# Three edits to the feed-forward stage of a one-core decoder layer: the rate of weight sums in DRAM, the place of one gate product, the order of one group of matrix products

## The chip, the core and the metric

The kernel is one program on one core of a Trainium2 chip. Five engines work side by side, each through its own instructions in order: TensorE (PE, matrix products; its weight loads are PEld), VectorE (DVE), ScalarE (ACT), GpSimd (POOL) and SyncE (SP, which here only issues transfers). Sixteen DMA engines move data between DRAM and the on-chip memory, and from DRAM to DRAM. The metric is the device time of one execution in microseconds (us); lower is better. Three executions of the kernel before took 1026.02, 1028.47 and 1030.43 us; the median is 1028.47 us.

## What is computed

One decoder layer on 512 tokens of 1024 channels in float32: a recurrent mixer and an attention mixer, merged by gates, and then a gated feed-forward block with a short convolution over time. The edits lie in the feed-forward block, which is this part of the reference:

```python
up = causal_dwconv(rms_norm(x, norm2_g) @ w_up, ffn_conv_w, ffn_conv_b)
gate, val = jnp.split(up, 2, axis=-1)
x = x + (jax.nn.gelu(gate) * val) @ w_down
```

Here x is 512 x 1024, w_up is 1024 x 6144, gate and val have 3072 channels each, and w_down is 3072 x 1024. The convolution has three taps per channel.

## The kernel before

**Precision.** Every float32 operand is split into a rounded high part and a remainder (whi and wlo of a weight tile wraw, xh and xl of an activation), and a product is three matrix products: high by high, high by low, low by high. ACT makes the high part (line 202 for weights, line 264 for activations) and DVE the remainder (line 210 and line 265). So PE can't start the first product of a weight tile before ACT's copy, nor the third before DVE's subtraction. PE's order is written out by hand in this stage; the order on the other engines is set by a scheduler when the program is built, and at run time each engine keeps to that order: an instruction that waits holds up all that stands behind it.

**The up product.** The 3072 gate channels are 24 chunks of 128, and so are the value channels. Chunks 0 to 5 are done as plain products. Chunks 6 to 23 (the Strassen part) are done with a seven-product scheme on 2 x 2 blocks: gate and value of a chunk are the two block rows, the two halves of the 1024 input channels the inner blocks, 256 tokens a block column. `seed(j)` does four of the products (weight tiles u1 and u2 of chunk j), `rest(j)` the other three (u3 and u4), and the PE order is seed(j+1), rest(j), seed(j+2), and so on. Block sums of activations (b11, t1 to t4, b21, b22) are made once; block sums of weights are not made by an engine, but in DRAM: `sums()` copies the blocks of chunk j into a DRAM tile ws (line 1267, issued by SP) and then adds to it three times by accumulating transfers (line 1270, issued by POOL). The down product needs sums too, in twelve DRAM tiles dn0 to dn11, one for each pair of chunks: one copy of 512 KB (line 1292, SP), then an accumulating transfer from the input "we" and one from dn to itself, 256 KB each (line 1270, POOL). Each of POOL's accumulating transfers waits for the transfer before it on the same tile to land.

**When the sums are issued.** `sums()` is a generator of steps; a copy is one step, the two or three accumulating transfers of a round are the next. `_wprep`, which issues the load of each weight tile in the order of a plan of 229 tiles (line 196, SP), takes further steps by a table: with SUM_RATE's entry (116, 1.2), one step for 1.2 weight tiles up to tile 116, after that one for 2.4. The Strassen part begins at tile 109 of the plan. A step is issued behind the load of its tile on SP.

**From up to down.** For each chunk, `conv` applies the taps (ACT line 1349, DVE line 1352) into two tiles y (four buffers), ACT applies the gelu (line 1451), and `gated` multiplies the two into f (line 1361): chunks 0 to 7 lie in f0, 8 to 15 in fxh, 16 to 23 in fxl. POOL does these products, in the same queue as its accumulating transfers, except the last one (chunk 23), which DVE does. `down_ops(n)` makes the operands of pair n, which joins chunks k and k + 4 (pair 3 joins 3 and 7): sums dt on DVE (lines 1494 to 1496), then the split into dh and dl. Pair 3 has a buffer of its own for dt, and the scheduler has put its DVE instructions into the Strassen part.

**The down product** has two phases. In phase one each of the 12 pairs gives four kinds of product (`one`, kinds a, c, d, e) into four output groups p = 0 to 3 (two PSUM banks each: r0 with halves lo and hi, r1 with halves lo and hi). Then `mix(p)` combines the four halves of a group: ACT copies r0 to ad, and DVE does four additions in place (lines 1555 to 1558; 1556 writes r0 hi, 1557 writes r1 lo, 1558 reads r1 lo and writes r1 hi). In phase two `two(p, n)` adds three more products for each pair: c into r1 lo, d into r0 hi, a into r0 lo.

Of the kernel before, what the change touches and what calls it, by code (L numbers as in the profile page):

```python
# [25 lines left out]
FC = D_FF // 128  # L26
# [37 lines left out]
    return k, k + 4  # L64


SUM_AT, SUM_RATE = 20, ((43, 0.65), (54, 2.0), (80, 4.0), (116, 1.2), (999, 2.4))
WLEAD = 2
ACC1, ACC2 = (0, 1, 2, 5, 8, 11), (0, 1, 2, 5, 8)

# [59 lines left out]
class Kern:  # L130
# [1207 lines left out]
    def ffn(self):  # L1338
        nc, ff = self.nc, self.ff
# [3 lines left out]
        fs = lambda j: f[j // 8][:, j % 8]  # L1343
# [11 lines left out]
        def plain(c):  # L1355
            ps = self.up0.pop(0) if self.up0 else self.proj("up", c)
            nc.vector.tensor_mul(ps, ps, self.rstd)
            return conv(ps, c)

        def gated(j, yg, yv):  # L1360
            (nc.vector if j == FC - 1 else nc.gpsimd).tensor_mul(fs(j), yg, yv)


        SB = {}
# [78 lines left out]
        def rest(j, r0, r1):  # L1443

            w = self.w("u3", j, WLEAD)
            prod(r0[:, 256:512], w, 0, "b22")
            prod(r0[:, 0:256], w, 512, "b21")
            w = self.w("u4", j, WLEAD)
            prod(r1[:, 0:256], w, 0, "t4")
            yg = conv(r0, j)  # L1450
            nc.scalar.activation(yg, yg, AF.Gelu_apprx_tanh)
            gated(j, yg, conv(r1, FC + j, True))

        with tp("xt", side="right") as xt:
            x = xt.tile([128, KO, S], F32, name="xs")
            steps = prep(x, xt)
            for j in range(NPL):
                yg = plain(j)
                nc.scalar.activation(yg, yg, AF.Gelu_apprx_tanh)
                next(steps, None)  # L1460
                gated(j, yg, plain(FC + j))
                next(steps, None)
            for _ in steps:
                pass
# [48 lines left out]
    def down(self, fs, first):  # L1513

        nc, fo = self.nc, self.fo
        N, lo, hi = FC // 2, slice(0, 256), slice(256, 512)
        banks = [self.ps.tile([128, S], F32, name="mm", bufs=self.mmb) for _ in range(7)]
        banks.append(self.ps.tile([128, S], F32, name="misc"))
        r = [(banks[i], banks[j]) for i, j in ((0, 1), (2, 3), (4, 7), (5, 6))]
        self.down_load(2)  # L1520
        X = {0: first, 1: self.down_ops(1, fs)}
        W = {}

        def mm(ps, w, o, x, i, start=False, stop=False):
            c = slice(o, o + 128)
            nc.tensor.matmul(ps, w[0][:, c], x[0][:, i], start=start, stop=False, skip_group_check=True)  # L1526
            nc.tensor.matmul(ps, w[0][:, c], x[1][:, i], start=False, stop=False, skip_group_check=True)  # L1527
            nc.tensor.matmul(ps, w[1][:, c], x[0][:, i], start=False, stop=stop, skip_group_check=True)  # L1528

        def get1(n):  # L1530
            if n not in X:
                X[n] = self.down_ops(n, fs)
            W[n] = self.w("d1", n, WLEAD), self.w("d2", n, WLEAD)

        def one(p, n, which="acde"):
            (w1, w2), x, (r0, r1), o = W[n], X[n], r[p], 128 * p
            last = n == N - 1
            for s in which:
                if s == "a":
                    mm(r0[:, lo], w1, o, x, 0, n == 0, last)  # L1540
                elif s == "c":
                    mm(r1[:, lo], w1, 512 + o, x, 1, n == 0, last)
                elif s == "d":
                    mm(r0[:, hi], w2, 512 + o, x, 2, False, last)
                else:
                    mm(r1[:, hi], w2, o, x, 3, False, last)

        def mix(p):
            r0, r1 = r[p]
            a, d, c, e = r0[:, lo], r0[:, hi], r1[:, lo], r1[:, hi]  # L1550
            with self.tc.high_priority(HPRI):
                ad = fo.tile([128, S], F32, name="ad", bufs=2)
                ac = fo.tile([128, 256], F32, name="ac", bufs=2)
                nc.scalar.copy(ad, r0)
                nc.vector.tensor_tensor(ac, c, ad[:, lo], ALU.add)
                nc.vector.tensor_tensor(d, d, ac, ALU.add)
                nc.vector.tensor_tensor(c, e, ac, ALU.add)
                nc.vector.tensor_tensor(e, c, ad[:, hi], ALU.add)  # L1558

        def get2(n):  # L1560
            X[n] = self.down_ops2(n, fs)
            w4 = self.w("d4", n, WLEAD)
            W[n] = self.w("d3", n, WLEAD), w4

        def two(p, n, which="cda"):
            (w3, w4), x, (r0, r1), o = W[n], X[n], r[p], 128 * p
            last = n == N - 1
            for s in which:
                if s == "d":
                    mm(r0[:, hi], w3, o, x, 1, False, last)  # L1570
                elif s == "a":
                    mm(r0[:, lo], w3, 512 + o, x, 0, False, last)
                else:
                    mm(r1[:, lo], w4, o, x, 2, False, last)

        def store(p, j, cs):
            m = p + 4 * j
            o = self.ff.tile([128, S], F32, name="y", bufs=4)
            for c in cs:
                if j:  # L1580
                    nc.vector.tensor_sub(o[:, c], self.xn[:, m, c], r[p][1][:, c])  # L1581
                else:
                    nc.vector.tensor_add(o[:, c], r[p][0][:, c], self.xn[:, m, c])  # L1583
                nc.sync.dma_start(self.out[:, m, c], o[:, c])

        get1(0)
        for p, which in ((0, "ac"), (1, "ac"), (2, "c"), (0, "de"), (1, "de"), (2, "ade")):
            one(p, 0, which)
        get1(1)
        for p, n in ((0, 1), (1, 1), (3, 0), (2, 1), (3, 1)):  # L1590
            one(p, n)
        for n in range(2, N):
            get1(n)
            for p in range(4):
                one(p, n)
                if n == N - 1:
                    mix(p)
        for n in range(N - 2):
            get2(n)
            for p in range(4):  # L1600
                two(p, n)
        get2(N - 2)
        two(0, N - 2)
        two(1, N - 2)
        get2(N - 1)
        for p in range(3):
            two(p, N - 1)
            store(p, 0, (slice(0, S),))
            store(p, 1, (slice(0, S),))
            if p < 2:  # L1610
                two(p + 2, N - 2)
        for s in "cda":
            two(3, N - 1, s)
            if s == "c":
                store(3, 1, (slice(0, S),))
        store(3, 0, (hi, lo))
# [174 lines left out]
```

## Time and profile before

The profiled execution took 1027.07 us in all, and its span from the first to the last instruction is 1025.3 us.

| | before |
|---|---|
| median of three executions | 1028.47 us |
| profiled execution / its span | 1027.07 / 1025.3 us |
| busy share: PE, PEld, DVE, ACT, POOL | 98%, 87%, 79%, 63%, 27% |
| mean granted TensorE clock | 0.994 |
| transfers issued by SP (queue q1) | 153.65 MB |
| transfers issued by POOL (queue q0) | 30.98 MB |

A row of the timeline reads: start in us, duration in us, engine, line, operation, out<-in, count, and in brackets how long the engine had been idle and what released it. A row of the waits reads: who waits, for whom, us in total, times, longest. A row of the stretches gives for each engine the busy time and the count of instructions in the stretch, then the granted TensorE clock (PEclk, 1.00 is full), the busy share of the 16 DMA engines (it can pass 1 by a little) and GB/s. "DMA to landing" is the time from the issue of a transfer to its completion. Lines are those of the kernel before.

### The profile page before, as it was taken

How to read it: one execution, taken by the hardware profiler on the slowest of the kernel's cores; microseconds unless marked ns; L12 is line 12 of the kernel's file. 1: busy time of each engine (PE TensorE's matmuls, PEld its weight loads, DVE VectorE, ACT ScalarE, POOL GpSimd, SP SyncE). 2: the span in 40 equal slices, each digit the busy share in tenths (PEclk: the TensorE clock that was granted, in tenths of full speed). 3: DMA queues.
4: the chain of work that ended last, by engine and by line, in shares of the span. 5: the costliest groups of instructions: out<-in, count | busy, mean ns of one | idle time of the engine just before them, and what ended most of it. 6: DMA issues, size and time to landing. Idle time of an engine off the chain costs nothing. (4 is left out here: it accounts for less than half of the span.)

```text
span 1025.3 us, 16991 instructions
## 1 busy us (share of the span) xinstructions
PE 1005.7 (98%) x6089; PEld 895.6 (87%) x6089; DVE 807.7 (79%) x1569; ACT 645.8 (63%) x1075; POOL 273.8 (27%) x350
## 2 busy tenths in 40 slices
PE   9999999999999999999999999999989999999998
PEld 7888888988888888888888878888989999999997
DVE  6868879788778687769598564599678888899876
ACT  6466776878867663578787543465446666665553
POOL 0155335334443400341332004234211111221000
PEclk9999999999999999999999999999999999999999
DMA  7534654665656677763645978668976656786553
GB/s 250 113 89 105 169 146 131 162 152 157 185 144 165 191 250 232 179 206 126 168 112 148 302 207 226 165 184 236 274 201 195 191 185 200 207 229 203 156 185 124
DMA packets 74933, 185.88 MB, mean 181 GB/s; under 512 B 18011, under 2 KB 19675, under 8 KB 71008
## 3 DMA queue, kind: packets, MB, share of 16 engines
q1 hardware_dynamic: 66064, 153.65, 45.0%
q0 software_dynamic: 8640, 30.98, 17.9%
q8 instruction: 48, 0.79, 0.3%
q14 instruction: 37, 0.30, 0.1%
q10 hardware_dynamic: 144, 0.15, 0.1%
HBM read 175.53 MB, written 57.93 MB: 228 GB/s over the span
## 5 line engine op out<-in xcount | busy, mean ns | idle before, releaser
L202 ACT CAST whi<-wraw 128x1024 fp32r<-128x1024 f32 (+3 forms) x178 | 177.9, 999 | 148.6 <-PE mm L1419 50.7
L210 DVE TENSOR_TENSOR wlo<-wraw,whi 128x1024 fp32r<-128x1024 f32 (+2 forms) x145 | 166.0, 1145 | 60.3 <-ACT whi L202 60.1
L239 PE MATMUL mm<-xh,whi 128*128 128x512 f32 x456 | 178.8, 392 | 0.0
L241 PE MATMUL mm<-xh,wlo 128*128 128x512 f32 x456 | 178.6, 392 | 0.0
L240 PE MATMUL mm<-xl,whi 128*128 128x512 f32 x456 | 178.3, 391 | 0.0
L207 POOL TENSOR_TENSOR wlo<-wraw,whi 128x256 fp32r<-128x256 f32 (+1 forms) x131 | 94.9, 777 | 100.7 <-ACT whi L202 82.3
L241 PEld LDWEIGHTS mm<-xh,wlo 128*128 128x128 f32 x456 | 85.6, 188 | 18.5
L239 PEld LDWEIGHTS mm<-xh,whi 128*128 128x128 f32 x456 | 85.7, 188 | 16.8
L240 PEld LDWEIGHTS mm<-xl,whi 128*128 128x128 f32 x456 | 85.7, 188 | 16.7
L929 ACT ACTIVATE s<-s,bs,rq 128x128 f32<-128x128 f32 (+3 forms) x128 | 82.4, 647 | 13.8 <-DVE bs L926 13.7
L1527 PE MATMUL mm<-dl,whi 128*128 128x256 f32 x300 | 84.0, 280 | 1.6 <-DVE dl L265 1.6
L1526 PE MATMUL mm<-dh,whi 128*128 128x256 f32 x300 | 84.0, 280 | 1.5 <-DVE mm L1558 1.5
L1528 PE MATMUL mm<-dh,wlo 128*128 128x256 f32 x300 | 83.9, 280 | 0.0
L265 DVE TENSOR_TENSOR ptl<-T,pth 128x512 fp32r<-128x512 f32 x80 | 55.0, 688 | 20.7 <-ACT pth L264 19.8
L264 ACT CAST pth<-T 128x512 fp32r<-128x512 f32 x80 | 46.2, 582 | 31.8 <-PE T L958 31.2
L1270 POOL DMA_DIRECT2D ws<-ws x36 | 28.5, 791 | 137.8 <-DMA ws<-in_wi 63.8
L922 DVE CUSTOM_DVE_ANT_0 s<-S,cc 128x128 f32<-128x128 f32 (+3 forms) x128 | 58.1, 482 | 2.8 <-PE S L919 2.4
L1527 PEld LDWEIGHTS mm<-dl,whi 128*128 128x128 f32 x300 | 56.5, 188 | 2.0 <-DVE dl L265 2.0
L1526 PEld LDWEIGHTS mm<-dh,whi 128*128 128x128 f32 x300 | 56.4, 188 | 1.9 <-DVE mm L1558 1.7
L1528 PEld LDWEIGHTS mm<-dh,wlo 128*128 128x128 f32 x300 | 56.4, 188 | 0.2 <-DVE wlo L210 0.2
L958 PE MATMUL T<-cc,s 128*128 128x128 f32 x320 | 48.2, 273 | 0.6 <-DVE s L934 0.6
L958 PEld LDWEIGHTS T<-cc,s 128*128 128x128 f32 x320 | 39.5, 140 | 10.2 <-DVE s L934 0.8
(439 smaller groups left out, 2874.1 us busy)
## 6 DMA issues: line engine op xcount, KB each, us to landing
wraw<-in_w SPq DMA_DIRECT2D x102, 512.0 KB, 3.6
ws<-in_wi SPq DMA_DIRECT2D x36, 512.0 KB, 5.0
wraw<-ws SPq DMA_DIRECT2D x72, 256.0 KB, 3.3
wraw<-in_w SPq DMA_DIRECT2D x54, 256.0 KB, 3.2
ws<-in_wa POOLq DMA_DIRECT2D x18, 512.0 KB, 6.0
ws<-ws POOLq DMA_DIRECT2D x36, 256.0 KB, 4.8
dn<-in_wd SPq DMA_DIRECT2D x12, 512.0 KB, 5.9
ds<-in_w SPq DMA_DIRECT2D x24, 256.0 KB, 3.4
```

The costliest lines, as they stand in the source:

```text
L202: self.last_hi = nc.scalar.copy(hi[:, :n], raw[:, :n])
L207: nc.gpsimd.tensor_sub(lo[:, e], raw[:, e], hi[:, e].bitcast(F32))
L210: self.last_lo = nc.vector.tensor_sub(lo[:, :e], raw[:, :e], hi[:, :e].bitcast(F32))
L239: nc.tensor.matmul(ps, wh, xh, start=first, stop=False)
L240: nc.tensor.matmul(ps, wh, xl, start=False, stop=False)
L241: nc.tensor.matmul(ps, wl, xh, start=False, stop=last)
L922: nc.vector.tensor_tensor_reduce(s[i, x], ps[:, x - xs[0]], mask, 1.0, -3e38, ALU.add, ALU.max, mx[:, x, i:i + 1])
L929: self.last_exp = nc.scalar.activation(s[t, x], s[t, x], AF.Exp, bias=bs[:, x, t:t + 1], scale=rq[:, t], accum_out=sm[:, x, t:t + 1])
L958: nc.tensor.transpose(T[:, off:off + 128], s[i, x][:, 128 * j:128 * j + 128], self.ident)
L1526: nc.tensor.matmul(ps, w[0][:, c], x[0][:, i], start=start, stop=False, skip_group_check=True)
L1527: nc.tensor.matmul(ps, w[0][:, c], x[1][:, i], start=False, stop=False, skip_group_check=True)
L1528: nc.tensor.matmul(ps, w[1][:, c], x[0][:, i], start=False, stop=stop, skip_group_check=True)
```

## The change

There are three edits. The steps of the sums are taken at 1.3 weight tiles a step up to tile 116 and at 2.8 after it, instead of 1.2 and 2.4. The gate product of chunk 23 is not issued on DVE where it is ready, but behind the remainder of the weight tile that is the latest when pair 2 of phase one is fetched (`issue_after` makes the scheduler place it behind that instruction). And in phase two, pair 0's products of each group run in the order a, d, c instead of c, d, a.

```diff
-SUM_AT, SUM_RATE = 20, ((43, 0.65), (54, 2.0), (80, 4.0), (116, 1.2), (999, 2.4))
+SUM_AT, SUM_RATE = 20, ((43, 0.65), (54, 2.0), (80, 4.0), (116, 1.3), (999, 2.8))
...
         def gated(j, yg, yv):
-            (nc.vector if j == FC - 1 else nc.gpsimd).tensor_mul(fs(j), yg, yv)
+            if j == FC - 1:
+                self.last_f = lambda: nc.vector.tensor_mul(fs(j), yg, yv)
+            else:
+                nc.gpsimd.tensor_mul(fs(j), yg, yv)
...
         for n in range(2, N):
             get1(n)
+            if n == 2:
+                with self.tc.issue_after(self.last_lo.ins):
+                    self.last_f()
             for p in range(4):
                 one(p, n)
...
             get2(n)
             for p in range(4):
-                two(p, n)
+                two(p, n, "cda" if n else "adc")
```

The three places below show how this moves instructions. Numbers behind a name tell buffers apart and differ between the two programs; in dn10 and ws10 the first number is that of the pair or chunk. Lines of the changed kernel are up to six higher.

First SP, in the Strassen part, where chunk 10's tiles are loaded. Before:

```order
L196 DMA wraw_7770<-in_w 128x512
L1292 DMA dn11_7774<-in_wd 16x8192
L196 DMA wraw_7809<-in_w 128x512
L196 DMA wraw_7809<-ws10_2506 128x512
L196 DMA wraw_7840<-ws10_2506 128x512 x2
```

and with the change:

```order
L196 DMA wraw_7766<-in_w 128x512
L196 DMA wraw_7803<-in_w 128x512
L196 DMA wraw_7803<-ws10_2506 128x512
L1292 DMA dn10_7808<-in_wd 16x8192
L196 DMA wraw_7836<-ws10_2506 128x512 x2
```

The copy for dn11 stood two transfers before chunk 10's first block sum; now the copy for dn10 stands behind it, and dn11's comes ten loads further on. The copies ahead of this place have moved by one pair: at about the places of dn7 to dn10 stand dn6 to dn9 now.

Second POOL, at the end of the same stretch, from the accumulating transfers of the last pairs to the first products of fxh. Before:

```order
L1361 TENSOR_TENSOR f0_6921<-y_7593,y_7598 128x512
L1270 DMA dn10_7640<-dn10_7640 32x2048
L1270 DMA dn11_7774<-in_we 32x2048
L1270 DMA dn11_7774<-dn11_7774 32x2048
L1361 TENSOR_TENSOR f0_6921<-y_7727,y_7732 128x512
L1361 TENSOR_TENSOR fxh_7378<-y_7859,y_7864 128x512
```

and with the change:

```order
L1364 TENSOR_TENSOR f0_6919<-y_7589,y_7594 128x512
L1270 DMA dn9_7636<-dn9_7636 32x2048
L1270 DMA dn10_7808<-in_we 32x2048
L1364 TENSOR_TENSOR f0_6919<-y_7723,y_7728 128x512
L1270 DMA dn10_7808<-dn10_7808 32x2048
L1364 TENSOR_TENSOR fxh_7374<-y_7855,y_7860 128x512
L1270 DMA dn11_8004<-in_we 32x2048
L1270 DMA dn11_8004<-dn11_8004 32x2048
```

The second product into f0 (chunk 7) stood behind three accumulating transfers after chunk 6's; it now stands behind two.

Third DVE, at the start of phase one of the down product. Before:

```order
L1494 TENSOR_TENSOR dt_9924<-f0_6921 128x256
L1361 TENSOR_TENSOR fxl_7379<-y_9762,y_9767 128x512
L1495 TENSOR_TENSOR dt_9924<-f0_6921 128x256
L1494 TENSOR_TENSOR dt_10071<-fxh_7378 128x256
L1496 SCALAR_TENSOR_TENSOR f0_6921<-dt_9924,f0_6921 128x256
L1495 TENSOR_TENSOR dt_10071<-fxh_7378 128x256
L210 TENSOR_TENSOR wlo_9857<-dg_9780,whi_9856 128x1024
L210 TENSOR_TENSOR wlo_9861<-ds_9781,whi_9860 128x1024
L265 TENSOR_TENSOR dl_9926<-f0_6921,dh_9925 128x512
L210 TENSOR_TENSOR wlo_9943<-dg_9798,whi_9942 128x1024
L265 TENSOR_TENSOR dl_9926<-dt_9924,dh_9925 128x512
```

and with the change, from the fifth of these on:

```order
L1498 TENSOR_TENSOR dt_10071<-fxh_7374 128x256
L265 TENSOR_TENSOR dl_9925<-dt_9923,dh_9924 128x512
L1499 SCALAR_TENSOR_TENSOR fxh_7374<-dt_10071,fxh_7374 128x256
L210 TENSOR_TENSOR wlo_9856<-dg_9779,whi_9855 128x1024
L210 TENSOR_TENSOR wlo_9860<-ds_9780,whi_9859 128x1024
L265 TENSOR_TENSOR dl_9925<-f0_6919,dh_9924 128x512
L210 TENSOR_TENSOR wlo_9942<-dg_9797,whi_9941 128x1024
L1336 TENSOR_TENSOR ds_9798<-ds_9798,dg_9797 128x512
L265 TENSOR_TENSOR dl_10000<-f0_6919,dh_9999 128x512
L265 TENSOR_TENSOR dl_10000<-dt_9998,dh_9999 128x512
L210 TENSOR_TENSOR wlo_9946<-ds_9798,whi_9945 128x1024
L1362 TENSOR_TENSOR fxl_7375<-y_9762,y_9767 128x512
```

The product into fxl has gone behind eight weight or operand remainders; the remainder of pair 1's dt (dl_9926, now dl_9925) comes ahead of the weight remainders, together with one sum of pair 4 (line 1496, now 1499) that stood further back.

## Prediction

> **What bounds the kernel now.** I began with the page's first lines, the span and the busy times.
>
> ```profile
> span 1025.3 us, 16991 instructions
> ...
> PE 1005.7 (98%) x6089; PEld 895.6 (87%) x6089; DVE 807.7 (79%) x1569; ACT 645.8 (63%) x1075; POOL 273.8 (27%) x350
> ```
>
> PE is busy for 98% of the span, and the change leaves its products as they are. So an edit can win only time in which PE waits or runs at a lower clock, some 20 us in all. Next I read what PE waits for from 700 us to the end, the part that the edits touch.
>
> ```profile
> PE mm L1420 <- DVE wlo L210: 4.4, 2, 3.7
> PE mm L1527 <- DVE dl L265: 1.6, 2, 0.9
> PE mm L1526 <- DVE mm L1558: 1.5, 1, 1.5
> PE mm L1418 <- ACT whi L202: 0.8, 1, 0.8
> ```
>
> Four rows, each answered by one edit. Lines 1418 and 1420 are the Strassen part (rate of the sums), 1527 the start of the down product (last gate product), 1526 the start of phase two (order a, d, c). What the Strassen waits really cost shows in the stretches around them: PE's count of products there, beside the calm stretch behind.
>
> ```profile
> 730.80:737.20 6.40, 4.90 (x26) 4.48 (x25) 4.88 (x6) 4.85 (x7) 0.00 (x0) 0.74 0.78 249
> 737.20:754.20 17.00, 17.00 (x148) 17.00 (x146) 12.54 (x19) 10.76 (x15) 4.74 (x6) 1.00 0.93 267
> 754.20:761.20 7.00, 3.35 (x17) 3.15 (x16) 5.14 (x8) 1.16 (x3) 1.79 (x2) 0.76 0.55 128
> 761.20:905.00 143.80, 143.78 (x1233) 143.58 (x1231) 124.36 (x181) 91.73 (x119) 24.90 (x19) 1.00 0.65 197
> ```
>
> In the last row a product takes 143.8/1233 = 0.117 us. So 26 products should take 3.0 us and took 6.4: the first stall cost 3.4 us, of which 1.5 is waiting (0.8, and 4.4 less 3.7) and the rest is the granted clock of 0.74. The 17 products of the second should take 2.0 and took 7.0: 5.0 us, 3.7 of it waiting.
>
> **The second stall (first edit).** What is late there is not a weight. I followed wlo back on DVE, then on POOL and on SP.
>
> ```profile
> 746.28 0.73 DVE L1352 SCALAR_TENSOR_TENSOR y<-mm,npw,y 128x510 f32<-128x510 f32 x1
> ...
> 750.25 0.43 DVE L1440 TENSOR_TENSOR mm<-mm,ad 128x256 f32<-128x256 f32 x1
> 756.02 0.42 DVE L1495 TENSOR_TENSOR dt<-f 128x256 f32<-128x256 f32 x1 [5.35 <-POOL f L1361]
> ```
>
> ```profile
> 746.95 0.80 POOL L1270 DMA_DIRECT2D dn<-dn  x1 [6.86 <-DMA dn<-in_we]
> 747.48 1.07 POOL L1270 DMA_DIRECT2D dn<-in_we  x1
> 753.94 0.76 POOL L1270 DMA_DIRECT2D dn<-dn  x1 [5.39 <-DMA dn<-in_we]
> 754.47 1.52 POOL L1361 TENSOR_TENSOR f<-y 128x512 f32<-128x512 f32 x1
> ```
>
> DVE's queue has pair 3's dt (line 1495) ahead of a weight remainder, and that dt needs f of chunk 7. The second y of chunk 7 was ready at 747.0 (746.28 + 0.73). But POOL stood at a transfer that waited 5.39 us for the one before it to land, and f came behind. So DVE idled 5.35 us and PE 3.7; the difference, 1.7 us, is what DVE may idle there before PE feels it.
>
> With the change f of chunk 7 stands behind one transfer fewer: after dn9 to itself (the place of 746.95) and "we" into dn10 (the place of 747.48). The long wait for that "we" to land no longer stands ahead of f. In its place the issue of "we" needs the copy into dn10, which SP now issues later. Where, and how long a copy took to land there:
>
> ```profile
> 737.74 0.49 SPq L1292 DMA_DIRECT2D dn<-in_wd  x1
> 741.21 0.33 SPq L196 DMA_DIRECT2D wraw<-in_w  x1
> 741.58 1.42 SPq L196 DMA_DIRECT2D wraw<-ws  x2
> ```
>
> ```profile
> DMA to landing us min/median/max: 6.5/8.2/9.0
> ```
>
> ```profile
> DMA to landing us min/median/max: 4.2/5.9/12.0
> ```
>
> The copy's new place is behind the first transfer of the row at 741.58, so at about 742.0. The second fence is of dn's three transfers issued from 734 to 738, the third of all twelve copies. With 8.2 it lands at 750.2, POOL issues "we", f starts 0.5 later (747.48 less 746.95) and ends at 752.2. DVE would idle from 750.7 (756.02 less 5.35) to 752.2, 1.5 us, just inside the 1.7. Ends: at 4.2 nothing is left of the stall (5.0 us won), at 12.0 f ends at 756.0 as before (nothing won). I take the whole 5.0, since the median of the fence nearest in time keeps inside the slack; a landing one us later costs one us of PE.
>
> **The first stall (same edit).** Here a load is late.
>
> ```profile
> 730.66 1.05 ACT L202 CAST whi<-wraw 128x1024 fp32r<-128x1024 f32 x1 [5.53 <-DMA wraw<-ws]
> ```
>
> ```profile
> DMA to landing us min/median/max: 9.5/11.5/11.7
> ```
>
> ```profile
> 700.42 0.78 POOL L1270 DMA_DIRECT2D dn<-dn  x1 [4.78 <-DMA dn<-in_we]
> ```
>
> ```profile
> 692.00:696.00 4.00, 4.00 (x19) 3.33 (x18) 4.00 (x5) 0.78 (x1) 2.87 (x2) 1.00 0.22 68
> 696.00:700.00 4.00, 4.00 (x20) 3.30 (x19) 4.00 (x5) 2.44 (x3) 0.00 (x0) 1.00 0.65 137
> 700.00:704.00 4.00, 4.00 (x19) 3.33 (x18) 4.00 (x6) 2.73 (x4) 1.41 (x2) 1.00 0.93 273
> ```
>
> ```profile
> q0 software_dynamic: 8640, 30.98, 17.9%
> ```
>
> Loads issued from 718 to 722 took 9.5 to 11.7 us (second fence), because the engines have been full since 700. By the order, SP's copies keep their places there and only carry a lower pair. On POOL one transfer leaves the full stretch: at 700.42 dn6 was added to itself; now dn5's is at the place of the "we" before it, when the share was 0.22 to 0.65. Queue q0 needs 17.9% of 1025.3 us for 30.98 MB, so 1.55 us for 0.262 MB. If all of that reaches the late load, both waits of 1.5 us and the slow clock go: 3.4 us. If the transfers behind merely move up and keep the queue as long: nothing. POOL's next transfers wait for landings and not for a time, so they move up too and refill a part of the room; I take half, 1.7.
>
> [...]
>
> **Last gate product.** DVE is the queue that PE waits for at 911.
>
> ```profile
> 905.86 0.69 DVE L1361 TENSOR_TENSOR fxl<-y 128x512 f32<-128x512 f32 x1
> ```
>
> ```profile
> 910.07 0.69 DVE L265 TENSOR_TENSOR dl<-f,dh 128x512 fp32r<-128x512 f32 x1
> 910.67 1.22 DVE L210 TENSOR_TENSOR wlo<-dg,whi 128x1024 fp32r<-128x1024 f32 x1
> 911.81 0.69 DVE L265 TENSOR_TENSOR dl<-dt,dh 128x512 fp32r<-128x512 f32 x1
> ```
>
> Ahead of the first dl one product leaves (0.69) and two rows come in, the remainder of dt (0.69) and a sum of 256 columns (0.42, as in the row of 756.02). So dl from f comes 0.4 later, and the longer of PE's two waits (0.9) grows to 1.3; the dl from dt is done by then, and the other (0.7) vanishes. That wins 0.3. The product itself has moved behind eight remainders, and its reader is the last pair but many us away. Ends: 0.7 won if the new rows find DVE's pipe free, 0.4 lost if ACT's copy of dt is late and both waits stay.
>
> **Order a, d, c.** PE waits once, in the last group.
>
> ```profile
> 971.36 0.42 DVE L1556 TENSOR_TENSOR mm<-mm,ac 128x256 f32<-128x256 f32 x1
> ...
> 972.36 0.43 DVE L1558 TENSOR_TENSOR mm<-mm,ad 128x256 f32<-128x256 f32 x1
> ```
>
> ```profile
> 972.84 0.38 PE L1526 MATMUL mm<-dh,whi 128*128 128x256 f32 x1 [1.48 <-DVE mm L1558]
> ```
>
> Product c needs line 1558, which sets 972.84 in both orders. But d needs only line 1556 (done at 971.8), a only ACT's copy. So six products, 6 x 0.117 = 0.7 us, move from behind c into the wait of 1.48. Ends: 0.7, or 0 if PE's wait holds them all.
>
> **The sum.** 5.0 + 1.7 + 0.3 + 0.7 = 7.7 us. The profiled execution took 1027.07 (span 1025.3 and 1.8 around it), which gives 1019.4. It lay 1.4 below the median of 1028.47; I add that back: 1020.8.
>
> **Rivals.**
>
> *The wait only changes hands* (0.20). The copy into dn10 lands after 12 us, f of chunk 7 ends at 756 as before, and the first stall stays. For it: the copy is issued 4.3 us later than dn11's was, and 12.0 has happened. Against it: the loads around are thinner by one copy. Left are 0.3 + 0.7: 1027.5.
>
> *The gain is given back* (0.14). PE comes to the next tiles 5 us earlier, while the share is still 0.93, and the copies and sums of dn10 and dn11 now fall into what followed:
>
> ```profile
> 760.00:764.00 4.00, 4.00 (x31) 4.00 (x31) 3.93 (x8) 2.16 (x3) 1.29 (x1) 0.86 0.83 278
> ```
>
> A load is late once more at the price of the first stall, 3.4, which itself stays: 1028.5 - 5.0 - 1.0 + 3.4 = 1025.9. Against it: behind 761 the mean share is 0.65, and one pair's transfers there come over 14 us (two steps of 2.8 tiles; a chunk has four tiles and 84 products, 9.8 us).
>
> *Slower* (0.08). The new wait feeds itself: a late copy makes f late, PE late, SP's next loads late, and dn11's copy stands in that queue. With a landing of L us PE loses L less 8.4; that passes the old 3.7 at 12.1, eats the other edits' 1.0 at 13.1, and is 0.5% slower from 18.2. Place: line 1495 at 750 us. No copy has taken over 12.0. Its time would be 1034.
>
> **The numbers.** Forecast 1020.8, chance 0.58, its own range 1017.5 to 1023. The low end is the sum with the first stall gone (9.4 won, 1019.1) less the spread of some 2 us that three executions show. The high end takes in the two rivals on the side of no change. A difference under 0.5% (5 us) can't be told from none. Faster is the forecast, 0.58; same is 0.20 + 0.14; slower 0.08.
>
> **What would show it.** Right: in the waits the row of line 1420 shrinks from 4.4 to under 1.5, DVE's idle time before line 1495 from 5.35 to under 2, no stretch from 750 to 762 has a clock under 0.9, and the row of line 1526 falls to 0.8 or less. The second rival: DVE waits for f as long as before, with POOL idle before "we" into dn10. I'd be wrong if new rows of whi or wlo appear between 760 and 800.

## The result, and the profile after

Six executions of the changed kernel took 1018.43 to 1021.62 us, median 1018.84; six of the kernel before on the same chip had a median of 1029.13. The medians differ by 10.3 us. The ratio, which is that of the means, is 0.9907 (95% interval 0.9887 to 0.9927): 9.5 us faster, the interval going from 7.5 to 11.6. The forecast was 1020.8. The profiled execution took 1018.66 us, 8.4 under the profiled one of before. The page's first lines:

```profile
span 1016.9 us, 16996 instructions
...
PE 1002.1 (99%) x6089; PEld 891.7 (88%) x6089; DVE 809.9 (80%) x1569; ACT 645.0 (63%) x1075; POOL 273.7 (27%) x350
```

What PE waits for from 700 us to the end (lines of the changed kernel are three higher: 1423 was 1420, 1529 and 1530 were 1526 and 1527):

```profile
PE mm L1530 <- DVE dl L265: 1.2, 1, 1.2
PE mm L1529 <- DVE mm L1559: 0.7, 1, 0.7
PE mm L1423 <- DVE wlo L210: 0.4, 1, 0.4
```

Of 8.3 us of waiting 2.3 are left. The stretches that held the two stalls, in the same columns as before:

```profile
730.80:737.20 6.40, 6.40 (x55) 6.22 (x54) 6.37 (x10) 4.73 (x7) 2.42 (x3) 1.00 0.92 268
737.20:754.20 17.00, 16.64 (x143) 16.43 (x142) 16.18 (x22) 10.13 (x14) 4.11 (x5) 1.00 0.94 272
754.20:761.20 7.00, 7.00 (x63) 7.00 (x62) 6.12 (x10) 4.69 (x7) 1.29 (x1) 1.00 0.98 309
```

In the first, 55 products are done where 26 were, in the third 63 where 17 were, both at full clock. DVE, POOL and SP at the second stall's place:

```profile
749.17 0.42 DVE L1443 TENSOR_TENSOR mm<-mm,ad 128x256 f32<-128x256 f32 x1
749.51 0.41 DVE L1498 TENSOR_TENSOR dt<-f 128x256 f32<-128x256 f32 x1
```

```profile
744.73 0.80 POOL L1270 DMA_DIRECT2D dn<-dn  x1 [7.12 <-issue]
746.06 0.78 POOL L1270 DMA_DIRECT2D dn<-in_we  x1 [0.54 <-DMA dn<-in_wd]
746.61 1.55 POOL L1364 TENSOR_TENSOR f<-y 128x512 f32<-128x512 f32 x1
751.76 0.80 POOL L1270 DMA_DIRECT2D dn<-dn  x1 [3.61 <-DMA dn<-in_we]
```

```profile
739.79 0.55 SPq L1292 DMA_DIRECT2D dn<-in_wd  x1
```

DVE takes pair 3's dt (now line 1498) without any idle time, where it had waited 5.35 us. POOL's f of chunk 7 stands behind a wait of 0.54 us for dn10's copy; the next landing is waited for only behind f. And ACT's late load at the first stall:

```profile
729.51 1.05 ACT L202 CAST whi<-wraw 128x1024 fp32r<-128x1024 f32 x1 [3.31 <-DMA wraw<-ws]
```

ACT waited 3.31 us there instead of 5.53, and PE not at all. One new row, however, lies far ahead of the edits:

```profile
PE mm L241 <- DVE wlo L210: 1.8, 1, 1.8
```

It is at 375 us, in the attention output, where the kernel before waited 0.4. Whether it comes from the change had to be found out.

### The profile page after: what moved, and what is told of

Its sections match the earlier page's. It is cut to its first block, busy times and chain, and to the rows that moved or that the text cites. A ratio compares the mean times of both kernels' runs of the same rounds, so it can differ in the third digit from the quotient of the medians.

```text
span 1016.9 us, 16996 instructions
## 1 busy us (share of the span) xinstructions
PE 1002.1 (99%) x6089; PEld 891.7 (88%) x6089; DVE 809.9 (80%) x1569; ACT 645.0 (63%) x1075; POOL 273.7 (27%) x350
## 4 chain that ended last, share of the span: by engine, by line
PE 75%; DVE 11%; DMA 6%; ACT 4%; issue 3%; SPq 0%; POOL 0%; DVEq 0%; ACTq 0%
PE mm L241 11%; PE mm L240 11%; PE mm L239 11%; PE mm L1423 5%; PE mm L1422 5%; PE mm L1421 5%; PE O L949 4%; DMA wraw<-in_w 4%; PE T L958 3%; PE mm L1529 3%; PE mm L1530 3%; PE mm L1531 3%; DVE wlo L210 2%; PE S L918 2%; PE S L919 1%
## 5 line engine op out<-in xcount | busy, mean ns | idle before, releaser
L210 DVE TENSOR_TENSOR wlo<-wraw,whi 128x1024 fp32r<-128x1024 f32 (+2 forms) x145 | 168.6, 1163 | 57.8 <-ACT whi L202 57.7
```

The costliest lines, as they stand in the source:

```text
L210: self.last_lo = nc.vector.tensor_sub(lo[:, :e], raw[:, :e], hi[:, :e].bitcast(F32))
```

## The experiments

PE runs the same products in the same order in all kernels but for the order of pair 0 in phase two, so the time from one product to another can be compared across traces. The table gives, for the one profiled execution of each run (the runs are numbered e1 to e11 and described below), the time between the products that the kernel before runs at the times in the heading. Without a stall the first stretch (153 products of 0.117 us) takes 17.9 us and the second (148) 17.3.

| profiled kernel | 726.1 to 747.5 (first stall) | 747.5 to 770.1 (second stall) | 900.1 to 918.0 | 970.0 to 980.1 |
|---|---|---|---|---|
| before | 21.46 | 22.56 | 17.92 | 10.02 |
| edits 2 and 3 (e5) | 19.42 | 22.07 | 17.22 | 9.43 |
| order only (e6) | 18.56 | 23.15 | 19.46 | 9.43 |
| last product only (e7) | 19.03 | 25.00 | 17.22 | 10.02 |
| f of chunk 7 on DVE (e4) | 19.12 | 17.40 | 17.93 | 10.09 |
| four transfers less (e9) | 17.85 | 25.31 | 17.74 | 10.02 |
| rate 1.3 / 2.4 (e3) | 19.48 | 20.93 | 17.97 | 10.09 |
| rate 1.2 / 2.8 (e2) | 19.74 | 17.27 | 17.97 | 10.02 |
| rate 1.3 / 2.8 (e1) | 19.32 | 17.27 | 17.98 | 10.09 |
| changed | 18.10 | 17.90 | 17.27 | 9.35 |
| changed, again (e10) | 17.85 | 17.27 | 17.22 | 9.43 |
| changed, gates split (e8) | 18.49 | 17.27 | 17.28 | 9.35 |
| changed, gates split, again (e11) | 18.99 | 17.69 | 17.28 | 9.36 |

### The rate alone

```diff
-SUM_AT, SUM_RATE = 20, ((43, 0.65), (54, 2.0), (80, 4.0), (116, 1.2), (999, 2.4))
+SUM_AT, SUM_RATE = 20, ((43, 0.65), (54, 2.0), (80, 4.0), (116, 1.3), (999, 2.8))
```

> The kernel before with the first edit alone (steps at 1.3 and 2.8 weight tiles). Theory: both stalls of the Strassen part go (5.0 + 3.4 us by the stretches of the kernel before), the waits at the start of the down product (0.9 and 0.7) and of phase two (1.5) stay: about 8.4 us under the kernel before. Rival, that the other two edits carry a good part: with the sum of the prediction for this edit, 5.0 + 1.7 = 6.7, or less, and the row of the up product's waits still there. The two differ by 1.7 us in time, but plainly in the rows of the waits and in the granted clock from 730 to 761.

Median 1019.77 against 1028.1 (23 executions), ratio 0.992 (0.9896 to 0.9945): 8.3 us faster. Most of the gain is this edit's. The waits of the other two edits stayed (1.6 and 1.5 us); the row of line 1420 fell to 0.8 us, as two short waits. That the time agrees with the 8.4 of the theory is in part luck: only the second stall is gone in the table (17.27 us), while the first stretch still took 19.32 us, so the first stall did not go.

### Its second number alone

```diff
-(116, 1.2), (999, 2.4))
+(116, 1.2), (999, 2.8))
```

> The kernel before with only the second number changed (2.4 to 2.8), so that the one transfer in which dn11 is added to itself comes behind the gate product of chunk 7 on POOL, and nothing before about 730 us moves. Theory (that product stood behind POOL's wait for a landing): the second stall goes, 5.0 us, the first stays with its two waits near 731 and a clock under 0.8 there; about 5 us under the kernel before. Rival (both stalls are one thing, the load of the DMA engines from 700 on): neither goes, within 1 us of the kernel before, since the transfers until 740 are the same.

Median 1019.85, ratio 0.9927 (0.9903 to 0.9951): 8.2 us faster, as much as both numbers together. POOL at the place:

```profile
745.08 0.80 POOL L1270 DMA_DIRECT2D dn<-dn  x1 [4.30 <-DMA dn<-in_we]
749.05 0.77 POOL L1270 DMA_DIRECT2D dn<-in_we  x1 [3.17 <-DVE mm L1439]
749.58 1.59 POOL L1361 TENSOR_TENSOR f<-y 128x512 f32<-128x512 f32 x1
754.82 0.80 POOL L1270 DMA_DIRECT2D dn<-dn  x1 [3.65 <-DMA dn<-in_we]
```

f stands ahead of dn11's transfer to itself, and DVE's wait for it was 0.84 us, within the slack. The rival falls. But the theory missed too: the first stall should have stayed, and its stretch took 19.74 us and not 21.46, although no transfer ahead of that stretch had moved.

### Its first number alone

```diff
-(116, 1.2), (999, 2.4))
+(116, 1.3), (999, 2.4))
```

> The kernel before with only the first number changed (1.2 to 1.3): one accumulating transfer fewer between 700 and 730 us, as in the changed kernel, but the gate product of chunk 7 stands behind dn10's transfer to itself, whose wait for a landing was 5 to 7 us in the rows. Theory: the first stall goes (3.4 us), the second stays at 3 to 5 us; 2.5 to 4.5 us under the kernel before. Rival (a thinner load before 730 heals both): 8.4 us under it, and DVE's wait before line 1495 under 2 us.

Median 1026.34, ratio 0.9989 (0.9973 to 1.0006): no change that can be told. f stands behind dn10's transfer to itself:

```profile
752.80 0.76 POOL L1270 DMA_DIRECT2D dn<-dn  x1 [6.77 <-DMA dn<-in_we]
753.33 1.53 POOL L1361 TENSOR_TENSOR f<-y 128x512 f32<-128x512 f32 x1
```

```profile
754.89 0.42 DVE L1495 TENSOR_TENSOR dt<-f 128x256 f32<-128x256 f32 x1 [5.11 <-POOL f L1361]
```

```profile
756.97 0.38 PE L1420 MATMUL mm<-t1h,wlo 128*128 128x256 f32 x1 [3.34 <-DVE wlo L210]
```

The second stall stayed, with 3.34 us of PE, and DVE's wait of 5.11 us speaks against the rival. But half of the theory missed: the first stall did not go. Its stretch took 19.48 us, as long as in the kernels at 1.2 other than the profile before (18.56 to 19.74). So one transfer fewer in the full stretch did not heal the first stall here, and this run can't say what a healed one would be worth while the second stands.

### f of chunk 7 on DVE

```diff
-            (nc.vector if j == FC - 1 else nc.gpsimd).tensor_mul(fs(j), yg, yv)
+            (nc.vector if j in (7, FC - 1) else nc.gpsimd).tensor_mul(fs(j), yg, yv)
```

> The kernel before with the gate product of chunk 7 done on DVE instead of POOL (0.7 us there); no transfer changes its place in any queue. Theory: DVE no longer waits for POOL near 751, the second stall goes and the first stays, about 5 us under the kernel before. Rival (the sums near 750 are late for their readers, or the load of the engines holds the weight tiles up): another wait of the same length takes its place, within 1 us of the kernel before.

Median 1020.93, ratio 0.9935 (0.9908 to 0.9961): 7.2 us faster, with every transfer at its old place.

```profile
744.13 0.69 DVE L1361 TENSOR_TENSOR f<-y 128x512 f32<-128x512 f32 x1
744.74 0.42 DVE L1437 TENSOR_TENSOR ac<-mm,ad 128x256 f32<-128x256 f32 x1
745.08 0.41 DVE L1495 TENSOR_TENSOR dt<-f 128x256 f32<-128x256 f32 x1
```

POOL still waited 6.57 us for a landing at 751.81, but the next product behind it, chunk 8's at 753.63, then waited for DVE's y and not for POOL. That is the second stall's cause, shown from the other side. No other wait of that length took its place: the row of line 1420 is one wait of 0.8 us. The gain of 7.2 us is more than the second stretch accounts for (17.40 against 22.56 us), as it is in e2 (8.2 us, 17.27); the rest of both is not attributed.

### The other two edits

The changed kernel with the old rate; the order alone; the last product alone.

> The changed kernel with the old rate (1.2 and 2.4): the last gate product moved and the order a, d, c. Its up product is that of the kernel before, instruction for instruction, so this is a second look at both stalls. Theory: one wait of about 1.2 us at the start of the down product in place of two (1.6), one of 0.7 in place of 1.5 in phase two, so 1.2 us under the kernel before, too little to be told from none by the times; the second stall is there with over 3 us of waiting. On the first stall: if it is part of the kernel before, waits of 1.5 us near 731 with a clock under 0.8 show again; if it was a matter of that one execution, less than 1 us and full clock.

> The kernel before with the order a, d, c alone. Theory: the wait in phase two falls from 1.5 to 0.7 us, the two at the start of the down product stay at 0.9 and 0.7. Rival (PE's wait holds all six products up): 1.5 stays. Its up product is that of the kernel before, so it is also a third look at both stalls: the second with over 3 us of waiting, the first as under the edits without the rate.

> The kernel before with the last gate product moved alone. Theory: at the start of the down product one wait of about 1.2 us in place of 0.9 and 0.7, in phase two 1.5 as before. Rival (the second wait came from ACT and not from that product): 0.9 and 0.7 stay, or 1.3 and 0.7. A fourth look at both stalls.

Both edits without the rate: median 1025.88 against 1028.0, ratio 0.998 (0.9958 to 1.0001), as small as expected. The other two were run once each and took 1027.68 and 1027.98. Their waits, first both edits, then the order, then the last product:

```profile
PE mm L1423 <- DVE wlo L210: 4.1, 3, 3.1
PE mm L1530 <- DVE dl L265: 1.2, 1, 1.2
PE mm L1529 <- DVE mm L1559: 0.8, 1, 0.8
```

```profile
PE mm L1420 <- DVE wlo L210: 4.4, 2, 4.1
PE mm L1527 <- DVE dl L265: 1.6, 2, 0.8
PE mm L1526 <- DVE mm L1556: 0.8, 1, 0.8
```

```profile
PE mm L1423 <- DVE wlo L210: 5.4, 2, 4.7
PE mm L1529 <- DVE mm L1561: 1.5, 1, 1.5
PE mm L1530 <- DVE dl L265: 1.2, 1, 1.2
```

Each edit changes its own wait and no other. In the table the last product is worth 0.5 to 0.8 us at 900 to 918, the order 0.6 to 0.7 at 970 to 980 (the 19.46 of e6 is put down to a stretch at half clock, an estimate worked out below). In all three the second stall is there, with waits of 3.1, 4.1 and 4.7 us. The first is not what the profile before showed: 18.56 to 19.42 us, at full clock. Its 21.46 was a dear execution.

### Four transfers less ahead of the first stall

```diff
-            if 0 <= n - 1 < N:
+            if 0 <= n - 1 < N and n - 1 not in (6, 7):
                 add(self.ds[n - 1][0:32], a["we"][n - 1])
-            if 0 <= n - 2 < N:
+            if 0 <= n - 2 < N and n - 2 not in (6, 7):
                 add(self.ds[n - 2][32:64], self.ds[n - 2][0:32])
```

> The kernel before without the four accumulating transfers into dn6 and dn7 (their rows at 694.86, 700.42, 706.25 and 714.39 us), so the down product's sums of these two pairs are left out; 4 x 1.55 = 6.2 us of all DMA engines less ahead of the loads that are late near 731. Five profiles with the kernel before's transfers up to there took 21.46, 19.42, 18.56, 19.03 and 19.12 us for the products between 726.1 and 747.5 us of the kernel before; without any stall they would take 17.9. Theory (the accumulating transfers make those loads late): ACT waits for block sums of weights at 731 for 2 us less, and the products take 18.2 or less. Rival (the loads are late whatever the sums do, by their own traffic): 18.6 to 19.5. The second stall is there as before.

One execution took 1030.76 us (median of the kernel before: 1026.57). The first stretch took 17.85 us, without a stall (ACT's row comes first, then DVE's):

```profile
732.27 1.05 ACT L202 CAST whi<-wraw 128x1024 fp32r<-128x1024 f32 x1 [2.47 <-DMA wraw<-ws]
```

```profile
759.86 0.42 DVE L1495 TENSOR_TENSOR dt<-f 128x256 f32<-128x256 f32 x1 [8.42 <-POOL f L1361]
```

ACT waited 2.47 us where it had waited 3.3 to 5.5 in the six others with the transfers in place (before, e2, e4 to e7). The loads issued 4 to 8 us ahead of the stretch's first product took 7.1 to 8.3 us to land, median 7.8; in those six the median was 8.9 to 11.5. So the accumulating transfers do make those loads late. But PE gained nothing. It came earlier to the second stall, and POOL there waited for the landing ahead of f for 9.34 us:

```profile
757.76 0.77 POOL L1270 DMA_DIRECT2D dn<-dn  x1 [9.34 <-issue]
```

In the six kernels with that stall (before, e3, e5, e6, e7, e9) f of chunk 7 ended 27.3 to 29.9 us after the product that opens the first stretch, and 28.9 us after it in e9, where that stretch was shortest. In the two profiles of the changed kernel f ended after 21.4 and 21.7 us. This fits the view that POOL's landings set the end, and that PE waits at the second stall for what it wins at the first. It is not shown: e9 is one execution, and its landing of 9.34 us is the longest of all.

### The wait at 375 us

The changed kernel again, and one that makes four of the eight gates of the attention output behind the second weight tile there (once alone, once beside the changed kernel).

```diff
-        for k in range(KO):
-            nc.sync.dma_start(self.ma[:, k], self.mg["mga", k])
+        for k in range(4):
+            gate(k)
         for m in range(8):
             wt = self.w("ao", m)
+            if m == 1:
+                for k in range(4, KO):
+                    gate(k)
```

> The changed kernel and one more edit far ahead of the feed-forward stage: of the eight gates of the attention output (line 1009) only four are made before the first weight tile there and four after the second, so that the weight remainder for which PE waited 1.8 us at 375 us has four DVE instructions fewer ahead of it. Theory: that wait goes to under 0.5 us, and with it the half clock behind it, in most executions; 1.5 to 3 us under the changed kernel, so 1016 to 1017.5. Rival (what is late there is the landing of the gates, of which the first four are still ahead, or ACT's sigmoids now stand ahead of weights): the wait stays or a new one comes; 1018 to 1021.

> The changed kernel once more, beside the next one on the same chip. Theory: 7 to 10 us under the kernel before, no wait near 755; the wait of 1.8 us at 375 us that its first profile showed is a matter of the execution, between 0.2 and 2.5 us with or without a half clock behind it. Rival (that wait came with the change): it is there again at 1.5 us or more.

> The changed kernel with the attention output's gates made four before and four after the second weight tile, beside the changed kernel on the same chip. Theory: the products between 366 and 390 us take 23.4 us again against 23.6 to 27.7 in the others, so 1 to 3 us under the changed kernel in the median, and a narrower spread. Rival: within 0.5 us of the changed kernel, since what is gained at 375 is lost at the next load that is late.

The changed kernel again: 1017.05 against 1026.57, ratio 0.9893 (0.9855 to 0.993), and 0.3 us of waiting at 375 us. With the old rate that wait was 0.4 us in the profile before and 2.6 us in e9, whose edit lies far behind it. So the row of 1.8 was a matter of that execution. With the gates split the times were 1018.1 (ratio 0.989, 0.986 to 0.992) and 1016.62 (0.9885, 0.9848 to 0.9921). In its first profile the wait was gone; in the second it was back:

```profile
PE mm L241 <- DVE wlo L210: 1.6, 1, 1.6
```

That theory falls. Against the changed kernel beside it (1017.05) nothing is gained that can be told, and no version here beats the changed one.

## Why the prediction was right, and where it was off

**Second stall, 5.0 us.** Right in cause and nearly in size. Between the profiled executions the second stretch fell by 4.7 us; the mean of the four kernels with the old order on POOL (before, e5, e6, e7) is 23.2 and that of the two profiles of the changed kernel 17.6, so 5.6. The steps held: dn10's copy was to be issued at 742.0 and was at 739.79, PE being 2.7 us early by then; f was to end at 752.2 and ended at 748.16, or 750.9 with those 2.7 put back. The landing was over-estimated: POOL's "we" followed the copy's issue by 6.3 us, not 8.2. So DVE didn't idle at all, where 1.5 us had been allowed for; in the second profile, e10, it idled 1.38 us, with "we" 6.8 us behind the copy. PE did not wait for it in either, as the slack of 1.7 us had it.

**First stall, 1.7 us.** The term that was mis-sized, in both directions. Between the profiled executions the whole 3.4 us vanished. But 3.4 was not the usual price of this stall in the kernel before: the six profiles with its transfers up to there (before, e2, e4 to e7) have a mean of 19.6 us, 1.7 above the unstalled 17.9, and the five without the profile of before 1.3. The six profiles at 1.3 have 17.85 to 19.48, mean 18.7. So the edit is worth some 0.5 to 0.9 us there, of which the executions' own spread leaves little certain. The mechanism, accumulating transfers that make loads late, was shown by e9, but with four transfers, not with one; with one, e1 and e3 still had most of the stall (19.32 and 19.48 us). The step at fault was to price a stall from one execution. Whether the term may be added to that of a stall that follows it was not measured.

**The clock.** The sum took the slow clock as a fixed part of each stall's price. It is charged in some executions and not in others. The profile before, around both stalls, and the profile of e3, around its second one:

```profile
730.51:733.84 3.33, 1.83 (x14) 1.41 (x13) 1.88 (x2) 2.45 (x3) 0.00 (x0) 1.00 0.86 264
733.84:737.25 3.41, 3.41 (x19) 3.41 (x18) 3.05 (x4) 2.59 (x6) 0.04 (x1) 0.50 0.68 228
...
757.73:761.14 3.41, 3.04 (x14) 3.05 (x15) 3.41 (x6) 0.56 (x2) 0.00 (x0) 0.50 0.55 157
```

```profile
753.50:757.00 3.50, 0.16 (x3) 0.04 (x1) 2.07 (x4) 0.43 (x1) 1.36 (x2) 1.00 0.72 154
757.00:760.50 3.50, 3.50 (x30) 3.50 (x31) 3.50 (x5) 1.04 (x3) 0.80 (x1) 1.00 0.79 204
```

The clock is halved for 3.41 us at a time (before, 733.84 to 737.25 and 757.73 to 761.14), or for 6.82 us in e7 (757.63 to 764.45). In both traces the products there start 0.21 to 0.22 us apart where 0.117 is usual, so by estimate 3.41 us hold 16 of them and a halved stretch costs 3.41 less 16 x 0.117, some 1.5 us. e6's time from 900 to 918, 19.46 us against 17.74 to 17.98 in the other kernels with the old last product, is longer by about as much, which is why it is put down to one such stretch. After 1.5 us of waiting the kernel before had one such stretch; after 3.34 us in one piece e3 had none, at a clock of 1.00 from 750 to 764; e7 had two behind its 4.7. In the profile before they begin at 71.65, 733.84 and 757.73 us, 662.19 and 23.89 us apart, which is 194 and 7 times 3.413.

PE's busy time in the 3.41 us ahead does not tell which wait is charged. Ahead of a halved stretch it was 0.12 us (before, from 754.32), 0.52 (e5, from 749.43), 1.59 (changed, from 373.73), 1.83 in 3.33 us (before, from 730.51) and the whole 3.41 (before, from 68.24). In e3 it was 0.16 of the 3.50 us from 753.50, and the clock behind stayed at 1.00. So what a wait costs differs from execution to execution, and what decides it no run shows.

**Last gate product, 0.3 us.** Right by its steps: the second wait went and the first became 1.2 us (1.3 forecast). By the products it is worth 0.65, about twice the term; why more than the 0.4 us of waiting, no run shows.

**Order a, d, c, 0.7 us.** Right: 0.6 to 0.7, with d now waiting 0.7 us for line 1556 (now 1559).

**The sum.** 7.7 was forecast. Typical sizes from the table give 5.6 + 0.8 + 0.65 + 0.65 = 7.7. That the two sums agree is luck: one term was 0.9 too large, two were 0.6 and 0.35 too small. The means moved by 9.5 us and the medians by 10.3, with an interval from 7.5. What lies beyond 7.7 is not attributed. Outside the four stretches the profiled executions of the kernel before and of e5 to e7 took 950.7 to 955.3 us, and the two of the changed kernel 954.3 and 955.5, so the traces show no further gain there. All the signs named for being right came in the first profile: the row of line 1420 at 0.4 us, no idle time before pair 3's dt, full clock from 750 to 762, and 0.7 us in the row of phase two. The rivals: the wait did not change hands, no new wait of whi or wlo came between 760 and 800, and the longest landing of a dn transfer was 10.3 us, far from 18.2.

## What to carry to other kernels

Before a number in an issue rate is tuned, look at what stands behind each waiting instruction of the queue: here most of the gain came from one product that had stood behind a wait for a landing on POOL, and taking the product to DVE won about as much (7.2 us in e4, 8.2 to 8.3 in e2 and e1). Price a stall from several executions, since the same wait may or may not be charged a halved clock (the 3.7 us before was, the 3.34 of e3 was not). Two stalls in a row need not add up: in the one execution of a kernel with the first gone and the second left (e9), PE waited 6.3 us at the second, so mend the second first.

## What was not expected of the hardware

Halved stretches of the TensorE clock came also in places where nothing differed between the kernels; in the profile before also ahead of the edits:

```profile
71.65:75.06 3.41, 3.41 (x16) 3.41 (x15) 1.87 (x8) 1.93 (x4) 2.23 (x4) 0.50 0.39 136
```

The first profile of the changed kernel had none there, but one from 377.14 us on, behind the wait of 1.8. What decides whether a wait is charged is not settled. Right ahead of the halved stretch at 71.65 there was no wait at all: from 68.24 to 71.65 PE was busy for the whole 3.41 us, with 31 products, most of them narrow (8 of 2 columns, 12 of 64). And POOL waited between 5.39 and 9.34 us for the landing ahead of f in the five profiles with dn11's transfers ahead of it (before, e5, e6, e7, e9), so one and the same queue of waits ended some 4 us apart.
